# Hybrid decoder layer: memory keys computed by token, two pieces of x's last tiles split from PSUM, the first loads reordered

## The chip, the cores and the metric

The kernel runs on one core of a Trainium2 chip. The metric is the device time of one launch in microseconds, taken as the median of several runs. PE is the matrix engine (TensorE), PEld its weight loads, DVE the vector engine, ACT the scalar engine, POOL GpSimd, SP the engine whose queue issues most DMAs. SBUF is the working memory, PSUM holds the matmuls' results in eight banks.

## The reference

One layer of a decoder with three groups of heads that share one input projection, and a final norm. Sequence 1024, model width 2048, 256 memory tokens.

```
h = rmsnorm(x, ln_g)
proj = h @ w_in                      # columns of three groups
A: chunked causal gMLP gating        # 4 groups x 128
B: gated DeltaNet, 8 heads of 128    # short conv on q, k, v; chunked delta rule
C: cross-attention, 4 heads of 128:
   m = rmsnorm(mem, mem_norm_g)
   mk, mv = split(m @ w_mem_kv)      # keys, values: 256 tokens x 512 each
   p = softmax(cq @ mk.T / sqrt(128));  out = p @ mv
each group's output times silu of its own gate columns
x = x + concat(A, B, C) @ w_out
y = rmsnorm(x, final_g)
```

All of it is float32 and must come out that exactly: a product is made of three matmuls in the faster fp32r format, each operand split into a rounded part (hi) and the rest (lo): hi·hi, hi·lo, lo·hi.

## The kernel before

**The order of the work.** Every instruction is first recorded by `Plan.add`, with its dependences found from the memory regions it touches. `Plan.issue` then plays the whole program through a cost model: each engine takes, of the instructions that are ready by the model, the one with the lowest class (`rank(n)`, lower first), then the earliest in the code. `behind(op)` only tells the plan to wait for `op`. The order found is written out for each engine, and all instructions appear in the profile under line 300, so they are told apart by their tiles. On the chip each engine works its list strictly in that order and waits by semaphores.

**The first stage** computes the memory keys and values. `mem` is loaded in two tiles of 128 tokens, each in four pieces of 512 columns (`load_mem(q)` loads piece q of both; the tiles are `kT`, `qT` and their `w` twins). Seven dummy products (`warm(7)`) run on PE meanwhile. The norm weights `mem_norm_g` and `ln_g` come as 32 rows of 128 in one tile (`y1`, shown as `y`), and one PE transpose turns them into columns `gcol`. `spread_mem(q)` transposes piece q of both tiles on PE into one bank each, and splits it into hi (`gt`) and lo (`inv`). `w_mem_kv` is taken in 16 slices of 128 rows by 1024 columns (keys in the first 512, values in the rest); slice k goes into one of four buffers (`wraw`, `ut`), is scaled by its norm column and split into `whi` and `wlo`, two of each. Slice 0 is loaded and scaled in two halves, the value half first, and that half is issued on ACT's queue.

Each slice has two parts of products. For the values, `va[mt]`, memory tokens are the rows of the result: the memory tile is the stationary operand and 512 weight columns move. For the keys, `ka[h]`, the head's channels are the rows: 128 weight columns are stationary and 256 memory tokens move. `va` takes two PSUM banks (`dn0`, `dn1`), `ka` the four banks `acc0` to `acc3`. The other two (`dn2`, `dn3`, taken in turn by `spare()`) serve the transposes.

The norm of each memory token (`row_scale`, into `rm`) is applied at the end. For the values it is one number per row. For the keys, tokens lie along the free axis, so at slice 7 a product of a matrix of ones with a diagonal matrix spreads the 256 norms over all partitions (`rmb`). Keys and values then go to a DRAM buffer (`kv_d`) on POOL's queue, to be read back and split by the attention stage.

**x in the same stage.** While the slices are worked, the first half of x (tiles 0 to 3, `load_x`) is loaded into buffers that earlier work leaves. `prep` scales a tile by its row norm, piece by piece, and transposes a piece into a spare bank. `put0` multiplies it by the columns of `ln_g` (`times_g`, into `tn`), splits it into `ahi` and `alo`, and stores it to `h0_d`. For tiles 0 and 1 (`tt < H0`) it also runs a small f32 product for the decays (`decay_rows`, `first_ab`) into the unused half of a key bank.

**After it** the large projections run by a seven-product scheme (`first_product`, `seven`): its sums and differences of h are made by `left_sums`, which adds `ahi` and `alo` back together, and by `prep1` for the second half of x. The first of these products takes tiles 0 and 1 first, pieces 2 and 3, and then tiles 2 and 3. Near the end of the projections the attention stage loads keys (`mkT`) and values (`mv`) from `kv_d`.

Of the kernel before, what the change touches and what calls it, by code (L numbers as in the profile page):

```python
# [9 lines left out]
F32 = mybir.dt.float32  # L10
# [50 lines left out]
class Plan:  # L61
# [242 lines left out]
def kernel(  # L304
# [32 lines left out]
    def C(shape, name, dt=F32):  # L337
        return sb.tile(list(shape), dt, name=name, tag=name)[:]
# [72 lines left out]
    mhalf, rms = (C([P, NH], n) for n in ("mhalf", "rm"))  # L411
    rm = [rms[:, i : i + 1] for i in range(2)]
    col2 = C([P, 16], "col2")[:, 0:9]
    gcol, cw = C([P, 32], "gcol"), C([P, 96], "cw")
    jk = C([P, 2 * HT], "jk", mybir.dt.bfloat16)
    small = Ring("small", 8, [P, 8])
    acc = [ps.tile([P, HT], F32, name=f"acc{i}", tag=f"acc{i}")[:] for i in range(4)]
# [72 lines left out]
    x_rows = {}  # L490
    whole_of.update((t.tensor.name, t) for t in ring["ut"].bufs)

    def load_mem(q):
# [43 lines left out]

    turn["dn"] = 1
    warm(7)
    pt = acc[3]  # L540
    PE.transpose(pt[:, 0:32], rows[0:32], ident[0:32, 0:32])
    with rank(1):
        V.tensor_copy(gcol, pt[:, 0:32])

    def times_g(o, tp, q):
        V.tensor_tensor(out=o, in0=tp, in1=bc(gcol[:, 16 + 4 * q : 20 + 4 * q], P), op=ALU.mult)

    def spread_mem(q):
        h, l = (ring[t](F32R).rearrange("p (k n) -> p k n", k=4) for t in ("gt", "inv"))
# [35 lines left out]

    def put0(tt):
        def put(q, tp):
            t = tok(ring["tn"]())
            with rank(1):
                times_g(t, tp, q)  # L590
            with rank(2):
                split_to(ahq[q][:, tt], alq[q][:, tt], t, V)
            if tt < H0:
                decay_rows(first_ab(tt), q, t, False)
# [12 lines left out]
    for k in range(KT):  # L607
        mh, ml = mhl[k // 4]
        if k >= 4:
            with rank(3):  # L610
                load_kv(k)
        hi, lo = kvhi[k % 2], kvlo[k % 2]
        with rank(2):
            for sl in kv_parts(k)[::-1]:
                raw = kvraw[k % 4][:, sl]
                if k == 0:
                    V.tensor_scalar(hi[:, sl], raw, gcol[:, k : k + 1], None, op0=ALU.mult)
                else:
                    S.activation(hi[:, sl], raw, AF.Copy, scale=gcol[:, k : k + 1])
                V.scalar_tensor_tensor(lo[:, sl], raw, gcol[:, k : k + 1], hi[:, sl], op0=ALU.mult, op1=ALU.subtract)  # L620
        kk = k % 4
        for mt in range(2):
            sl = slice(mt * P, (mt + 1) * P)
            triple(va[mt], (mh[:, kk, sl], ml[:, kk, sl]), (hi[:, XW:], lo[:, XW:]), k == 0, k == KT - 1)
        for h in range(NX):
            sl = slice(h * P, (h + 1) * P)
            triple(ka[h][:, :NMEM], (hi[:, sl], lo[:, sl]), (mh[:, kk], ml[:, kk]), k == 0, False)
        kvmark.append(R.ops[-1])
        if k == 0:
            with behind(kvmark[-1]), rank(2):  # L630
                G.dma_start(abw[:, 0 : KT * 16].rearrange("p (k c) -> p k c", c=16),
                            w_in[:, C_AB : C_AB + 16].rearrange("(k p) c -> p k c", p=P))
        if k in (1, 4, 8):
            with behind(kvmark[-1]):
                mhl.append(spread_mem(len(mhl)))
        if k == 1:
            load_x(0, "vs", kvmark[1:2] * 4)
        if k == 3:
            for mt in range(2):
                V.tensor_copy(rm[mt], row_scale(mem_rows[mt]))  # L640
        if k == 4:
            load_x(1, "kd", kvmark[4:5] * 4)
        if k == 5:
            prep(0, put0(0), spare)
        if k == 7:

            dg, rmb = (ring["E"]()[:, 0:NMEM] for _ in range(2))
            for mt in range(2):
# [12 lines left out]
    kv_d = DT([2, NX, P, NMEM], "kvd")  # L661
    with rank(1):
# [3 lines left out]
    for h in range(NX):  # L666
        with rank(2.5):
            G.dma_start(kv_d[0, h], kfs[h])
    for mt in range(2):
        t = ring[("ai", "kd")[mt]]()  # L670
        with rank(1):
            S.activation(t, va[mt], AF.Copy, scale=rm[mt])
        with rank(2.5):
            G.dma_start(kv_d[1, :, :, mt * P : (mt + 1) * P].rearrange("h p e -> p h e"), tok(t))
    with rank(2):
        prep(3, put0(3), spare, (2, 3, 0, 1))
    sums0 = ring["xr"].bufs[1][:, 0:HT]
# [1048 lines left out]
    for n, (tag, to) in enumerate((("gt", mkT), ("inv", mv))):  # L1726
        for i in range(NX // 2):
            t = ring[tag](F32R).rearrange("p (h s m) -> p h s m", h=2, s=2)
            G.dma_start(t[:, :, 1].bitcast(F32), kv_d[n, 2 * i : 2 * i + 2].rearrange("h p m -> p h m"))
# [191 lines left out]
```

## Time and profile before

| | us |
|---|---|
| median of 3 runs | 1588.99 |
| lowest, highest | 1588.22, 1590.04 |
| profiled execution: its own time | 1590.5 |
| profiled execution: span from first to last instruction | 1588.7 |
| PE busy in the span | 1575.6 |
| DVE busy | 1287.4 |
| ACT busy | 1016.2 |

The share of TensorE's clock that was granted is 0.998 over the span. Rows of a timeline have the start and the duration in us, the engine, the operation, output<-inputs, the shape and the number of instructions merged into the row; in brackets the idle time before it, and what ended it. Matmuls overlap: a row's duration is longer than the distance to the next one's start, and that distance is what a matmul costs in a stream. Rows of the chain have start, length and number of instructions. Groups have the count, the busy time with the mean in ns of one, and the idle time before them. Rows of DMA issues have the count, the size and the median us from issue to landing. Rows of windows have the busy time and count of each engine (PE, PEld, DVE, ACT, POOL), the clock, the share of time in which the DMA engines were busy, and GB/s.

### The profile page before, as it was taken

The numbers are of one execution on the slowest core, as the hardware profiler recorded it, in microseconds if no ns is written. First come the engines' busy times: TensorE is split into PE (matmuls) and PEld (weight loads), VectorE is DVE, ScalarE is ACT, GpSimd is POOL, SyncE is SP. The second block draws the span as 40 slices with busy tenths as digits, with TensorE's granted clock in tenths as the row PEclk, the third lists the DMA queues.
The fourth block names the chain that finished last, engine by engine and source line by source line (L and its number), as shares of the span: only waits on it lengthen the run. The fifth ranks groups of instructions, "written<-read, shape, count | busy, mean of one in ns | idle before, by whom it ended". The sixth has DMA issues, their size and how long they took to land.

```text
span 1588.7 us, 25645 instructions
## 1 busy us (share of the span) xinstructions
PE 1575.6 (99%) x8762; PEld 1317.2 (83%) x8762; DVE 1287.4 (81%) x1961; ACT 1016.2 (64%) x2088; POOL 311.7 (20%) x513
## 2 busy tenths in 40 slices
PE   9999999999999999999999999999999999999997
PEld 8878888888888888888888888888888888888886
DVE  5868996989899998997988776777768788688775
ACT  6762685776656788866775667766566864344355
POOL 1200042332402424235343133121000000000001
PEclk9999999999999999999999999999999999999999
DMA  8988868988679868986779775798877779688646
GB/s 305 319 279 278 274 214 306 349 303 268 199 253 345 270 215 283 357 306 219 263 233 356 240 259 188 242 327 257 283 255 260 260 238 355 198 283 294 202 146 238
DMA packets 213219, 425.77 MB, mean 268 GB/s; under 512 B 23112, under 2 KB 58672, under 8 KB 213088
## 3 DMA queue, kind: packets, MB, share of 16 engines
q1 hardware_dynamic: 190464, 367.40, 68.9%
q0 software_dynamic: 21840, 55.40, 10.5%
q8 instruction: 69, 1.13, 0.3%
q10 hardware_dynamic: 784, 1.33, 0.2%
q14 instruction: 62, 0.51, 0.1%
HBM read 335.40 MB, written 88.11 MB: 267 GB/s over the span
## 4 chain that ended last, share of the span: by engine, by line
PE 98%; DMA 1%; DVE 0%; issue 0%; ACTq 0%; ACT 0%; POOLq 0%; POOL 0%; DVEq 0%
PE acc L300 69%; PE dn L300 29%; DMA wraw<-in_w_in_dram 0%; DMA wraw<-in_w_mem_kv_dram 0%; DVE alo L300 0%; DVE zl L300 0%; ACTq L300 0%; ACT y2w L300 0%; DVE tn L300 0%; DVE kd L300 0%; DVE vs L300 0%; DVE inv L300 0%; POOLq L1916 0%; POOL small L300 0%; DVE whi L300 0%
## 5 line engine op out<-in xcount | busy, mean ns | idle before, releaser
L300 PE MATMUL acc<-ahi,whi 128*128 128x512 f32 (+1 forms) x1328 | 455.6, 392 | 0.0
L300 PE MATMUL acc<-ahi,wlo 128*128 128x512 f32 (+1 forms) x904 | 355.0, 393 | 0.0
L300 PEld LDWEIGHTS acc<-ahi,whi 128*128 128x128 f32 x1328 | 247.8, 188 | 47.7
L300 ACT CAST ahi<-raws 128x1024 fp32r<-128x1024 f32 x141 | 147.9, 1049 | 86.7 <-PE dn L300 40.4
L300 PEld LDWEIGHTS acc<-ahi,wlo 128*128 128x128 f32 x904 | 170.0, 188 | 32.6 <-issue 0.2
L300 PE MATMUL acc<-alo,whi 128*128 128x512 f32 (+1 forms) x480 | 187.5, 391 | 0.0
L300 PE MATMUL acc<-ahi,zh 128*128 128x512 f32 x424 | 167.2, 394 | 0.0
L300 PE MATMUL acc<-ahi,zl 128*128 128x512 f32 x424 | 167.2, 394 | 0.0
L300 PE MATMUL acc<-alo,zh 128*128 128x512 f32 x424 | 167.1, 394 | 0.0
L300 ACT CAST whi<-wraw 128x1024 fp32r<-128x1024 f32 (+1 forms) x78 | 80.6, 1033 | 70.4 <-PE acc L300 42.8
L300 DVE TENSOR_TENSOR wlo<-wraw,whi 128x1024 fp32r<-128x1024 f32 (+1 forms) x78 | 93.6, 1200 | 25.5 <-ACT whi L300 22.0
L300 POOL TENSOR_TENSOR small<-small,mhalf 128x1 f32<-128x1 f32 x26 | 16.6, 643 | 491.1 <-DVE small L300 488.9
L300 DVE TENSOR_TENSOR alo<-raws,ahi 128x1024 fp32r<-128x1024 f32 x71 | 87.5, 1233 | 21.9 <-ACT ahi L300 21.7
L300 PEld LDWEIGHTS acc<-alo,whi 128*128 128x128 f32 x480 | 90.3, 188 | 17.4
L300 DVE TENSOR_TENSOR ahi<-raws,ahi 128x1024 fp32r<-128x1024 f32 x70 | 85.4, 1220 | 18.8 <-ACT ahi L300 17.3
L300 DVE TENSOR_TENSOR alo<-y,ahi 128x1024 fp32r<-128x1024 f32 x65 | 79.3, 1220 | 17.4 <-ACT ahi L300 17.1
L300 PEld LDWEIGHTS acc<-ahi,zl 128*128 128x128 f32 x424 | 79.7, 188 | 15.3
L300 PEld LDWEIGHTS acc<-ahi,zh 128*128 128x128 f32 x424 | 79.8, 188 | 15.3
L300 PEld LDWEIGHTS acc<-alo,zh 128*128 128x128 f32 x424 | 79.7, 188 | 15.2
L300 ACT CAST ahi<-y 128x1024 fp32r<-128x1024 f32 x65 | 68.2, 1049 | 37.3 <-PE dn L300 17.6
L300 PE MATMUL dn<-whi,ahi 128*128 128x512 f32 x232 | 77.6, 389 | 0.0
L300 PE MATMUL acc<-whi,ahi 128*128 128x512 f32 x216 | 73.6, 392 | 0.0
(582 smaller groups left out, 3744.8 us busy)
## 6 DMA issues: line engine op xcount, KB each, us to landing
wraw<-in_w_in_dram SPq DMA_DIRECT2D x80, 512.0 KB, 5.1
raws<-sa SPq DMA_DIRECT2D x61, 512.0 KB, 5.3
y<-in_w_in_dram SPq DMA_DIRECT2D x40, 512.0 KB, 5.2
wraw<-in_w_out_dram SPq DMA_DIRECT2D x32, 512.0 KB, 4.9
raws<-h0d SPq DMA_DIRECT2D x29, 512.0 KB, 6.0
y<-sa SPq DMA_DIRECT2D x27, 512.0 KB, 4.8
raws<-sd SPq DMA_DIRECT2D x42, 256.0 KB, 2.9
raws<-hTd SPq DMA_DIRECT2D x16, 512.0 KB, 5.2
```

The lines of the kernel that those rows point to most:

```text
L300: o.fn(*o.args, **o.kw)
```

## The change

- First loads: memory tile 0, piece 0; the memory norm; slice 0 of the weights in its two halves; only then tile 1's piece 0 and `ln_g`. The norm columns are made in two transposes: `gcol` (memory) at the start, `lcol` (`ln_g`) behind slice 0. Slice 0's key half is scaled and rounded on ACT, its value half stays on DVE. The sums of squares of the memory rows are planned behind slice 0.
- Keys by token: the keys are computed like the values, memory tile stationary, 512 key columns moving, into `acc0` and `acc1`. Their norm is then one number per row, so the spreading product goes. They are stored by token (`key_d`), and the attention stage transposes them on PE, four 128x128 blocks into each of two banks, before it splits them. The decays of tiles 0 and 1 get `acc2` and `acc3`.
- x's tiles 2 and 3, pieces 0 and 1: no `tn`, no store in `put0`. Each block of 128 is scaled by its column and rounded on ACT straight from the bank, and DVE makes the rest in one instruction. `left_sums` has hi + lo anyway and stores it to `h0_d`, and takes one more buffer there so that the sum stays whole for the store.
- x's tile 3 is loaded at slice 10, behind slices 9 and 10, where it was at slice 13, behind slices 10 to 12.

```diff
-    gcol, cw = C([P, 32], "gcol"), C([P, 96], "cw")
+    gcol, lcol, cw = C([P, 16], "gcol"), C([P, 16], "lcol"), C([P, 96], "cw")
...
+    grow = rows[32:48]
     with rank(2):
-        load_mem(0)
+        load_mem(0, 0)
         S.dma_start(mrow, mem_norm_g[0].rearrange("(c p) -> c p", p=P))
-        S.dma_start(rows[16:32], ln_g[0].rearrange("(c p) -> c p", p=P))
-        for k in range(4):
+        load_kv(0)
+        load_mem(0, 1)
+        S.dma_start(grow, ln_g[0].rearrange("(c p) -> c p", p=P))
+        for k in range(1, 4):
...
+    def columns(o, g, pt, i):
+        with rank(1):
+            PE.transpose(pt[:, 0:16], g, ident[i : i + 16, i : i + 16])
+            V.tensor_copy(o, pt[:, 0:16])
...
     def first_ab(tt):
-        return ka[tt][:, NMEM : NMEM + P]
+        return ka[2 + tt][:, 0:P]
...
         def put(q, tp):
+            if tt >= H0 and q < NQ // 2:
+                with rank(2):
+                    h, l = ahq[q][:, tt], alq[q][:, tt]
+                    for k in range(4):
+                        g = lcol[:, 4 * q + k : 4 * q + k + 1]
+                        S.activation(h[:, k], tp[:, k], AF.Copy, scale=g)
+                        V.scalar_tensor_tensor(l[:, k], tp[:, k], g, h[:, k], op0=ALU.mult, op1=ALU.subtract)
+                return
...
-                if k == 0:
+                if k == 0 and sl.start:
                     V.tensor_scalar(hi[:, sl], raw, gcol[:, k : k + 1], None, op0=ALU.mult)
...
-        for h in range(NX):
-            sl = slice(h * P, (h + 1) * P)
-            triple(ka[h][:, :NMEM], (hi[:, sl], lo[:, sl]), (mh[:, kk], ml[:, kk]), k == 0, False)
+        for mt in range(2):
+            sl = slice(mt * P, (mt + 1) * P)
+            triple(ka[mt], (mh[:, kk, sl], ml[:, kk, sl]), (hi[:, 0:XW], lo[:, 0:XW]), k == 0, k == KT - 1)
         kvmark.append(R.ops[-1])
         if k == 0:
+            with behind(kvmark[-1]):
+                columns(lcol, grow, acc[3], 32)
...
-        if k == 7:
-
-            dg, rmb = (ring["E"]()[:, 0:NMEM] for _ in range(2))
-            for mt in range(2):
-                V.tensor_scalar(dg[:, mt * P : (mt + 1) * P], ident, rm[mt], None, op0=ALU.mult)
-            pt = spare()
-            PE.matmul(pt[:, 0:NMEM], ones, dg, start=True, stop=True)
-            S.copy(rmb, pt[:, 0:NMEM])
...
+        if k == 10:
+            load_x(3, "qT", (kvmark[9], kvmark[9], kvmark[10], kvmark[10]))
         if k == 13:
-            load_x(3, "qT", (kvmark[10], kvmark[11], kvmark[11], kvmark[12]))
...
-        kfs = [t[:, i * NMEM : (i + 1) * NMEM] for t in et for i in range(2)]
-        for h in range(NX):
-            V.tensor_tensor(out=kfs[h], in0=ka[h][:, :NMEM], in1=rmb, op=ALU.mult)
...
+    for mt in range(2):
+        with rank(1):
+            V.tensor_scalar(et[mt], ka[mt], rm[mt], None, op0=ALU.mult)
         with rank(2.5):
-            G.dma_start(kv_d[0, h], kfs[h])
+            G.dma_start(key_d[mt], et[mt])
...
-        V.tensor_tensor(out=a, in0=d, in1=a, op=ALU.subtract)
-        for i, t in ((1, a), (0, d), (2, c)):
+        b = a
+        if tt >= H0:
+            Q.dma_start(rows_of(h0_d, q, tt), twos_of(a))
+            b = room()
+        V.tensor_tensor(out=b, in0=d, in1=a, op=ALU.subtract)
+        for i, t in ((1, b), (0, d), (2, c)):
...
+            if n == 0:
+                G.dma_start(raw, key_d[:, :, i * NMEM : (i + 1) * NMEM].rearrange("t p c -> p t c"))
+                d = dnr()
+                with rank(1.5):
+                    for h in range(2):
+                        for m in range(2):
+                            PE.transpose(d[:, (2 * h + m) * P : (2 * h + m + 1) * P], raw[:, m, h * P : (h + 1) * P], ident)
+                src = d.rearrange("p (h m) -> p h m", h=2)
...
-                split_to(t[:, :, 0], t[:, :, 1], t[:, :, 1].bitcast(F32), V)
+                split_to(t[:, :, 0], t[:, :, 1], src, V)
```

More of the change, by code (lines that the diff above doesn't have):

```diff
@@ L491, with load_mem @@
     whole_of.update((t.tensor.name, t) for t in ring["ut"].bufs)
-    def load_mem(q):
-        for mt in range(2):
+    def load_mem(q, *mts):
+        for mt in mts or range(2):
             Q.dma_start(mem_rows[mt][q], mem[mt * P : (mt + 1) * P, q * HT : (q + 1) * HT])
@@ L539 @@
     warm(7)
[L540 to L543, printed above, removed]
+    def columns(o, g, pt, i):
+        with rank(1):
+            PE.transpose(pt[:, 0:16], g, ident[i : i + 16, i : i + 16])
+            V.tensor_copy(o, pt[:, 0:16])
+    columns(gcol, mrow, acc[3], 0)
     def times_g(o, tp, q):
-        V.tensor_tensor(out=o, in0=tp, in1=bc(gcol[:, 16 + 4 * q : 20 + 4 * q], P), op=ALU.mult)
+        V.tensor_tensor(out=o, in0=tp, in1=bc(lcol[:, 4 * q : 4 * q + 4], P), op=ALU.mult)
     def spread_mem(q):
@@ L593, in put @@
             if tt < H0:
-                decay_rows(first_ab(tt), q, t, False)
+                decay_rows(first_ab(tt), q, t, q == 0)
             with rank(5):
@@ L638 @@
         if k == 3:
-            for mt in range(2):
-                V.tensor_copy(rm[mt], row_scale(mem_rows[mt]))
+            with behind(kvmark[0]):
+                for mt in range(2):
+                    V.tensor_copy(rm[mt], row_scale(mem_rows[mt]))
         if k == 4:
@@ L655 @@
             load_x(2, "kT", (kvmark[6], kvmark[7], kvmark[7], kvmark[8]))
+        if k == 10:
+            load_x(3, "qT", (kvmark[9], kvmark[9], kvmark[10], kvmark[10]))
         if k == 13:
-            load_x(3, "qT", (kvmark[10], kvmark[11], kvmark[11], kvmark[12]))
             with rank(2):
                 prep(2, put0(2), spare, (2, 3, 0, 1))
-    kv_d = DT([2, NX, P, NMEM], "kvd")
-    with rank(1):
-        kfs = [t[:, i * NMEM : (i + 1) * NMEM] for t in et for i in range(2)]
-        for h in range(NX):
-            V.tensor_tensor(out=kfs[h], in0=ka[h][:, :NMEM], in1=rmb, op=ALU.mult)
-    for h in range(NX):
+    kv_d = DT([NX, P, NMEM], "kvd")
+    key_d = DT([2, P, XW], "keyd")
+    for mt in range(2):
+        with rank(1):
+            V.tensor_scalar(et[mt], ka[mt], rm[mt], None, op0=ALU.mult)
         with rank(2.5):
-            G.dma_start(kv_d[0, h], kfs[h])
+            G.dma_start(key_d[mt], et[mt])
     for mt in range(2):
@@ L673 @@
         with rank(2.5):
-            G.dma_start(kv_d[1, :, :, mt * P : (mt + 1) * P].rearrange("h p e -> p h e"), tok(t))
+            G.dma_start(kv_d[:, :, mt * P : (mt + 1) * P].rearrange("h p e -> p h e"), tok(t))
     with rank(2):
@@ L1728 @@
             t = ring[tag](F32R).rearrange("p (h s m) -> p h s m", h=2, s=2)
-            G.dma_start(t[:, :, 1].bitcast(F32), kv_d[n, 2 * i : 2 * i + 2].rearrange("h p m -> p h m"))
+            raw = t[:, :, 1].bitcast(F32)
+            if n == 0:
[6 more added lines that the diff above has]
+                src = d.rearrange("p (h m) -> p h m", h=2)
+            else:
+                G.dma_start(raw, kv_d[2 * i : 2 * i + 2].rearrange("h p m -> p h m"))
+                src = raw
             with rank(1.5):
-                split_to(t[:, :, 0], t[:, :, 1], t[:, :, 1].bitcast(F32), V)
+                split_to(t[:, :, 0], t[:, :, 1], src, V)
             to += [t[:, 0], t[:, 1]]
```

1 line of the change is left out of this document (removed).

## The prediction

> **What bounds the kernel now.** I read the first page first: the busy shares, then the chain of work that ended last.
>
> ```profile
> span 1588.7 us, 25645 instructions
> PE 1575.6 (99%) x8762; PEld 1317.2 (83%) x8762; DVE 1287.4 (81%) x1961; ACT 1016.2 (64%) x2088; POOL 311.7 (20%) x513
> PE 98%; DMA 1%; DVE 0%; issue 0%; ACTq 0%; ACT 0%; POOLq 0%; POOL 0%; DVEq 0%
> ```
>
> The matrix engine is busy 99% of the span and makes up 98% of the chain. A busy matmul row is not by itself proof that the engine could do no more, so I read next whom it waited for, over the whole run.
>
> ```profile
> PE dn L300 <- POOL ones L300: 1.1, 1, 1.1
> PE dn L300 <- DVE whi L300: 0.8, 1, 0.8
> PE dn L300 <- DVE ai L300: 0.6, 1, 0.6
> PE dn L300 <- DVE tn L300: 0.3, 1, 0.3
> PE dn L300 <- DVE inv L300: 0.2, 1, 0.2
> ```
>
> This is every wait of PE for another engine: 3 us in 1589, and two of the five lie in the first 8 us. So DVE, ACT, POOL and the DMA queues have nothing to give except where they make PE wait. The change is worth what it does to (1) the start, (2) the time PE needs for the same work and (3) these waits. The start, in order of time:
>
> ```profile
> 1.06 3.36 PE L300 MATMUL dn<-ones 128*128 128x128 f32 x14 [1.06 <-POOL ones L300]
> 4.52 0.45 PE L300 MATMUL dn<-ident,kT 128*128 128x128 f32 x1
> 5.08 0.28 PE L300 MATMUL acc<-ident,y 32*128 32x32 f32 x1
> 5.99 1.06 PE L300 MATMUL dn<-ident,qT 128*128 128x128 f32 x4
> 7.24 0.88 DVE L300 TENSOR_SCALAR whi<-wraw,gcol 128x512 fp32r<-128x512 f32 x2 [1.64 <-DMA wraw<-in_w_mem_kv_dram]
> 7.87 1.19 PE L300 MATMUL dn<-whi,gt 128*128 128x512 f32 x2 [0.82 <-DVE whi L300]
> 9.50 1.05 PE L300 MATMUL dn<-ones 128*128 128x128 f32 x4
> 12.27 0.63 PE L300 MATMUL dn<-wlo,gt 128*128 128x512 f32 x1
> 12.70 0.63 PE L300 MATMUL dn<-whi,inv 128*128 128x512 f32 x1
> 14.69 0.39 PE L300 MATMUL dn<-whi,inv 128*128 128x512 f32 x1
> 14.92 0.39 PE L300 MATMUL dn<-wlo,gt 128*128 128x512 f32 x1
> ```
>
> Dummies run until 4.4, then the transposes of the two memory tiles (kT, qT) and of the norm rows (y), then a hole up to the first product at 7.87, because the weight slice had not landed. The columns also show two rates: at 12 us a 512-wide matmul starts 0.43 us after the one before (12.70 - 12.27), at 15 us 0.23 us after (14.92 - 14.69). PE starts at about half rate and reaches the full one between 12.7 and 14.7; I take 13.5. The holes between 4 and 8 us add up to 1.0 us (4.42 to 4.52, 4.97 to 5.08, 7.05 to 7.87), and every us in which the full rate comes sooner is worth half a us.
>
> **The change, part by part.** Sums are against this profiled execution, whose span is 1588.7 and whose own time is 1590.5; the runs' median is 1588.99, so I carry the difference over to the median.
>
> *First loads.* What was issued when, and how long each took to land:
>
> ```profile
> 1.72 0.45 ACTq L300 DMA_DIRECT2D wraw<-in_w_mem_kv_dram  x1
> qT<-in_mem_dram SPq DMA_DIRECT2D x1, 256.0 KB, 4.5
> wraw<-in_w_mem_kv_dram ACTq DMA_DIRECT2D x1, 256.0 KB, 5.4
> wraw<-in_w_mem_kv_dram SPq DMA_DIRECT2D x1, 256.0 KB, 5.2
> y<-in_mem_norm_g_dram ACTq DMA_DIRECT2D x1, 8.0 KB, 3.3
> y<-in_ln_g_dram ACTq DMA_DIRECT2D x1, 8.0 KB, 3.7
> 2.00:4.25 2.25, 2.25 (x12) 2.12 (x10) 0.00 (x0) 1.28 (x1) 0.97 (x1) 1.00 0.85 203
> 4.25:7.00 2.75, 2.53 (x10) 1.69 (x9) 0.19 (x1) 1.31 (x3) 0.00 (x0) 1.00 1.01 370
> ```
>
> The third load of ACT's queue is issued at 1.72; each takes about 0.45 to issue, so on both queues the first go out near 0.8, the second near 1.25. Then the memory norm lands at 4.1, ln_g at 4.95, the second memory tile at 5.75, the key half of the weights at 6.9 and the value half at 7.1. The value half was third on ACT's queue, behind ln_g, which landed 0.85 us after the norm. In the new order it is second there, the key half is second on SP's, and the second memory tile comes after them. The last two columns of the window rows (DMA share, GB/s) say how soon they can land: 457 KB moved by 4.25, then 370 GB/s with the engines full. First tile and weight slice are 786 KB, so not before 5.1; shared with the second tile I take 5.6. Then 0.44 us of DVE and 0.16 of signal: first product near 6.3, not 7.87. But the four transposes of the second tile (1.06 us), which lay in the wait, now fall beside or behind that product, and a hole of about half a us before it remains, since the first tile's own transposes end near 5.7. The work stays the same, so this gains only what the holes shrink: from 1.0 to some 0.6 us, worth 0.2 (at half rate) to 0.4. The rest hangs on the clock: if the full rate comes as much sooner as the first product does (1.5 us), that is 0.75 more. Ends: 0 (loads only trade places on full DMA engines) and -2.0. I take -0.8, a little under the 1.0 of both together, because the transposes behind the first product may keep the unbroken work from starting as early. The key half of the first slice is rounded on ACT beside DVE's value half, and the memory norms' sums of squares wait for the first slice: ACT is off the chain, and they are read at 67 us. No cost.
>
> *Keys by token.* Per slice, twelve 256-wide matmuls become six 512-wide ones. The chain shows both in this stage:
>
> ```profile
> 28.51 1.43 PE acc L300 x12
> 29.94 1.38 PE dn L300 x6
> ```
>
> -0.05 us per slice; fifteen slices at full rate make -0.7 (ends 0 and -1.1). The row of norms spread over partitions goes: one f32 product, two DVE scalings, one ACT copy.
>
> ```profile
> 38.85 0.70 PE L300 MATMUL dn<-E,ones 128*128 128x256 f32 x2
> 39.48 0.43 PE L300 MATMUL acc<-tn,abw 128*32 128x128 f32 x8
> ```
>
> -0.6 (39.48 - 38.85; ends -0.45 and -0.8). The separate transpose of ln_g, a small f32 step between the first slice's products, adds 0.25 (0 to 0.4). The four key evictions on DVE become two, and six POOL stores four: off the chain. In exchange the keys must be turned round later: eight f32 128x128 transposes in two groups. Their price, from such a group between products:
>
> ```profile
> 117.40 0.66 PE L300 MATMUL dn<-ident,kTw 128*128 128x128 f32 x4
> 117.81 0.48 PE L300 MATMUL dn<-ahi,gt 128*128 128x512 f32 x1
> 118.13 0.40 PE L300 MATMUL dn<-ahi,whi 128*128 128x512 f32 x1
> ```
>
> Four take 0.41 us, and the product after them 0.32 where 0.23 is usual: 0.5 per group, +1.0 in all (0.8 to 1.3). Where do they stand? They use two banks that the scan holds last:
>
> ```profile
> 1165.94 1.03 PE L300 MATMUL dn<-ident,vs 128*128 128x128 f32 x8
> 1198.33 0.64 PE L300 MATMUL dn<-gt,xa 128*128 128x256 f32 x4
> ```
>
> The scan leaves the banks near 1168, the keys are first used at 1198: 30 us for a chain of some 5. Nobody waits, but the PE time itself is not hidden.
>
> *Two pieces of x's last tiles.* For tiles 2 and 3 and pieces 0 and 1, one DVE scaling into `tn`, one ACT cast and one DVE subtraction become four ACT and four DVE steps of 128 straight from the bank, and four h0 stores move on SP's queue to the place where `left_sums` has the rows anyway, with four more buffers from a ring of seven.
>
> ```profile
> L300 ACT ACTIVATE vs<-dn,hs 128x128 f32<-128x128 f32 x64 | 18.8, 368 | 8.4 <-issue 6.0 <-PE dn L300 2.4
> L300 DVE SCALAR_TENSOR_TENSOR steps<-dn,sc,vs 128x128 f32<-128x128 f32 x56 | 17.3, 344 | 6.0 <-PE dn L300 4.5 <-ACT vs L300 1.3
> L300 DVE TENSOR_TENSOR tn<-dn,gcol 128x512 f32<-128x512 f32 x16 | 10.6, 686 | 3.0 <-PE dn L300 3.0
> 76.56 1.26 PE L300 MATMUL dn<-ident,qT 128*128 128x128 f32 x8 [0.35 <-DVE tn L300]
> ```
>
> DVE pays 4 x 0.34 = 1.4 as before (two steps of 0.69), ACT 4 x 0.37 in place of one cast. The bank is held longer, about 2 us and not 0.7. These pieces come last of their tile and their halves are not multiplied for tens of us, so what covers it is the 12 matmuls per weight block that PE has ready; were those gone, each piece could cost 1.3 us. What it may remove is the wait in the last row: there PE has no product left until tile 3 is split, and x's tile 3 is now asked for three slices earlier. -0.35 (0 to -0.6).
>
> Sum: -0.8 - 0.7 - 0.6 + 0.25 + 1.0 - 0.35 = -1.2 us. Median 1588.99 - 1.2 = 1587.8.
>
> **The clock.** The Trainium skill, "TensorE: Matmul & The Clock Gate", Part 1, says that the array starts at half clock and is released after a busy window of about 3.4 us which runs freely, so that the point differs from run to run. The trace agrees with two rates, not with 3.4 us from the first matmul: the half rate lasts to about 13.5, some 5.6 us past the first product. By that rule the step would move by a whole window or not at all: for the clock's part of the start an estimate of 0 or -1.7 us (half of 3.4), where the sum has a value between.
>
> **Rivals.**
> A. *The full rate comes much sooner.* PE works without a hole from about 6.3, and the step falls 3 us or more earlier: -1.5 to -2 for the start, and with the other terms near their good ends (keys -0.9, norm row -0.7, turning +0.9, last wait -0.5) about -3.2: 1585.8. For it: the half rate is the largest loss in the profile. Against it: the dummies, four of them still at 9.5, did not bring it about before. Chance 0.19.
> B. *The start is hidden anyway.* DMA engines full at 1.01 give the same bytes by the same time, or the second tile's transposes, now behind the first product, break the stretch after which the full rate comes, and the step stays at 13.5. Then -0.2 for the start and nearly nothing from the rest (-0.7 - 0.6 + 0.25 + 1.0, with or without the last wait): 1588.4 to 1588.7. Against it: ln_g's 0.85 us ahead of the value half. Chance 0.13. The same page of the Trainium skill, Part 4, says that transposes do not count as busy for the clock; no run here shows it yet, and it would bring about the second of these ways.
> C. *Slower: PE stands at the key transposes.* PE's order is written out by the planner; if it puts them behind the scan's last transposes but ahead of the reads of those banks (two ACT reads, some 0.7 us each with signals about 1 us), PE stops twice for 1 us. It decides from 1.2 us of stop on: 1587.8 + 2.1 = 1589.9, and more if a neighbouring product is dragged along. Against it: PE was stopped by such things for 1.1 us in all after 10 us. Chance 0.09.
> The forecast has the remaining 0.59.
>
> **How the numbers follow.** A measurement of this kernel can tell about 0.2% from no change, 3.2 us: faster means below 1585.8, slower above 1592.2. Half of A and a little of the forecast's tail lie below: 0.16. Of C about half: 0.05. Range: 1585.2 (A with all good ends) to 1590.0 (C, or all bad ends: 0 - 0 - 0.45 + 0.4 + 1.3 - 0 = +1.2), some 0.1 left out on each side; the forecast's own is 1586.3 to 1589.0.
>
> **What would show it.** First product near 6.3 to 7.2; the start-to-start time falling from 0.42 to 0.23 before 13; six and six 512-wide matmuls per slice; no f32 product at 38 us; eight `ident` transposes between 1168 and 1198 without idle time before them; no wait of PE for `tn` at 76. I am wrong if PE's waits after 20 us grow by more than 2 us, or if the rate steps up at another point than the start of work explains.

## Result, and the profile after

The changed kernel takes 1591.63 us (median of 21 runs, 1589.29 to 1594.82), the kernel before 1589.40 in the same session (21 runs, 1587.85 to 1590.89): a ratio of 1.0014, 95% interval 1.0007 to 1.002. That is 2.2 us longer where 1.2 us shorter was forecast. By the forecast's own bound of 0.2% it is no change; the time lies above its range, and the interval excludes a gain.

The page of the changed kernel: span, busy engines, shares of the chain of waits by engine.

```profile
span 1591.7 us, 25469 instructions
PE 1574.1 (99%) x8673; PEld 1310.5 (82%) x8673; DVE 1284.1 (81%) x1965; ACT 1019.6 (64%) x2100; POOL 312.8 (20%) x511
PE 88%; DMA 6%; DVE 3%; issue 2%; ACT 0%; POOL 0%; DVEq 0%; POOLq 0%; SPq 0%; ACTq 0%
```

PE has 89 instructions less and is busy 1.5 us less (1575.6 before), yet the span is 3.0 us longer: PE stands longer. The chain says so too: 98% PE before, 88% now, with DMA and DVE in between. Whom PE waited for (us in total, times, longest), without the rows of the dummies (1.1) and of the norm rows (0.3) in the first 5 us:

```profile
PE dn L300 <- DVE whi L300: 2.0, 1, 2.0
PE acc L300 <- ACT whi L300: 1.9, 1, 1.9
PE acc L300 <- DVE y2w L300: 0.7, 1, 0.7
PE dn L300 <- DVE inv L300: 0.5, 1, 0.5
PE dn L300 <- ACT kdw L300: 0.5, 1, 0.5
PE dn L300 <- DVE tn L300: 0.4, 1, 0.4
PE dn L300 <- DVE ai L300: 0.3, 1, 0.3
PE acc L300 <- DVE wlo L300: 0.2, 1, 0.2
```

The first row is the hole before the first product. All others lie after 20 us: 4.5 us, where the kernel before had 1.1 (ai 0.6, tn 0.3, inv 0.2). The forecast named a growth by more than 2 us as the sign that it is wrong; it is 3.4. The largest, at 164 us, with the step of DVE and the cast of ACT that it hangs on:

```profile
164.18 0.96 DVE L300 TENSOR_TENSOR wraw<-kTw,wraw 128x768 f32<-128x768 f32 x1
165.23 0.83 ACT L300 CAST whi<-wraw 128x768 fp32r<-128x768 f32 x1 [6.05 <-DVE wraw L300]
166.12 0.50 PE L300 MATMUL acc<-ahi,whi 128*128 128x512 f32 x1 [1.89 <-ACT whi L300]
```

In the kernel before the same addition stood at 161.03 and PE did not wait. The start:

```profile
4.91 0.66 PE L300 MATMUL dn<-ident,kT 128*128 128x128 f32 x4
7.55 0.64 PE L300 MATMUL dn<-whi,gt 128*128 128x512 f32 x1 [1.98 <-DVE whi L300]
7.99 1.05 PE L300 MATMUL dn<-ident,qT 128*128 128x128 f32 x4
8.69 0.77 PE L300 MATMUL dn<-wlo,gt 128*128 128x512 f32 x1
...
10.97 0.46 PE L300 MATMUL acc<-wlo,gt 128*128 128x512 f32 x1
11.27 0.39 PE L300 MATMUL acc<-whi,inv 128*128 128x512 f32 x1
```

and the value half of the first weight slice (KB, us from issue to landing):

```profile
wraw<-in_w_mem_kv_dram ACTq DMA_DIRECT2D x1, 256.0 KB, 5.6
```

The first product comes at 7.55 in place of 7.87, not at 6.3: the value half, now second on ACT's queue (issued at 1.25), takes 5.6 us and lands at 6.85. The transposes of the second memory tile (qT) now come behind that product and take 0.70 us there (8.69 - 7.99). The full rate begins near 11.1 here, 13.8 in the profile before (a first stretch at full rate, from 4.27 to 7.68 us, falls for the most part into the hole). The eight key transposes stand where the forecast put them, without idle time:

```profile
1170.82 0.60 PE L300 MATMUL dn<-ident,gt 128*128 128x128 f32 x4
1171.17 0.71 PE L300 MATMUL acc<-ahi,whi 128*128 128x512 f32 x2
...
1172.42 0.60 PE L300 MATMUL dn<-ident,gt 128*128 128x128 f32 x4
1172.77 0.48 PE L300 MATMUL acc<-ahi,wlo 128*128 128x512 f32 x1
```

### The profile page after: what moved, and what is told of

Same layout as the page of the kernel before. It is cut to its first block, busy times and chain, and to the rows that moved or that the text cites. A ratio compares the mean times of both kernels' runs of the same rounds, so it can differ in the third digit from the quotient of the medians.

```text
span 1591.7 us, 25469 instructions
## 1 busy us (share of the span) xinstructions
PE 1574.1 (99%) x8673; PEld 1310.5 (82%) x8673; DVE 1284.1 (81%) x1965; ACT 1019.6 (64%) x2100; POOL 312.8 (20%) x511
## 4 chain that ended last, share of the span: by engine, by line
PE 88%; DMA 6%; DVE 3%; issue 2%; ACT 0%; POOL 0%; DVEq 0%; POOLq 0%; SPq 0%; ACTq 0%
PE acc L300 61%; PE dn L300 27%; DMA wraw<-in_w_in_dram 3%; DMA y<-in_w_in_dram 1%; DMA gt<-in_x_dram 1%; DVE wlo L300 1%; DVE alo L300 0%; DMA pd<-y 0%; DVE zl L300 0%; DVE wraw L300 0%; DMA kdw<-in_w_in_dram 0%; DMA kTw<-in_w_in_dram 0%; DMA wraw<-in_w_mem_kv_dram 0%; DVE kT L300 0%; DVE qT L300 0%
## 5 line engine op out<-in xcount | busy, mean ns | idle before, releaser
L300 ACT CAST ahi<-y 128x1024 fp32r<-128x1024 f32 x65 | 68.2, 1050 | 39.0 <-PE dn L300 17.8
```

The lines of the kernel that those rows point to most:

```text
L300: o.fn(*o.args, **o.kw)
```

## Reading all traces together

Two executions of one kernel differ by up to 6 us here, so one pair of profiles doesn't settle 2 us. For each kernel of the table (all that were run but e1 and e2), the same PE instructions were matched with those of the profile before (by names and shape, counted from the end), and the median of their differences in time taken in a few stretches. "Full from" is where the trace's clock records begin the long stretch at full rate; "corrected" takes the clock out of the column at 130-150 us (half of the difference in "full from": a product takes 0.42 us before it and 0.23 after it).

```
kernel                     full from  130-150  corrected  215-380  1100-1140   end
before                       13.76      0.00      0.00      0.00      0.00     0.00
e7  before, more PE work     12.38      0.65      1.34      0.65     -1.24    -1.24
e10 two pieces               9.93     -1.10      0.81     -1.14     -1.23    -1.23
e11 tile 3                   13.29      1.17      1.40      1.19      2.66     2.66
e15 first loads              11.39     -0.94      0.25     -0.94     -1.70    -1.70
e9  keys                      9.32      0.18      2.40      0.33     -0.11     0.81
e3  loads, keys              13.30      1.37      1.60      2.24      2.49     3.40
e4  all but loads            11.30     -1.79     -0.56      0.53     -0.15     0.77
changed                      11.10     -0.35      0.98      1.82      2.17     3.09
e12 changed, again           10.67     -1.36      0.18      0.62     -0.10     0.82
e13 changed, no turning      11.08     -1.02      0.32      0.62      0.72     0.72
e5  changed, old mid order   10.51     -1.84     -0.22     -0.48     -1.61    -0.70
e6  before, new mid order    10.36     -1.02      0.68      2.81      4.45     4.47
e8  changed, more PE work    10.04      0.32      2.18      1.08      1.31     2.22
e14 changed, early kTw       11.38     -0.65      0.54      4.62      5.73     6.64
e16 all but keys             13.24      2.95      3.21      2.92      3.80     3.80
e17 changed, early loads     11.52     -1.22     -0.10      1.18      1.40     2.32
e18 before, longer wait       9.53      2.34      4.45      2.34      2.42     2.42
```

The correction can be tested: e7 is the kernel before with 12 transposes more, and its corrected offset is 1.34 where 1.3 was expected; e6 and e18, in which nothing is changed up to 100 and 75 us, stand at +0.13 and +0.18, corrected, between 30 and 60 us. The larger values in the corrected column are mostly PE's waits up to there: 1.72 us in e11, 1.85 in e3 and 2.57 in e9, where the kernel before has 0.35. A profile stands for one execution only: that of e11 ends 2.66 late, its median just 0.2.

## The experiments

Each is given with its edit, the expectation on record, its median with the ratio to the kernel before in the same session (95% interval), and what follows. Theory 1 was at first that the parts save what was forecast and that the planner's new order of everything downstream loses it; theory 2 that the parts themselves cost; theory 3, formed after e4, that PE comes sooner to work that DVE and the loads set, and waits there.

**The order of instructions (e1, e2, e5, e6).** The planner writes its order by `o.at`; here a list written out takes its place.

```
-        self.ops.sort(key=lambda o: (o.at, o.idx))
+        self.ops.sort(key=lambda o: place[o.idx])
```

> The changed kernel, but every instruction behind the start is issued in the place that the planner gave it in the kernel before (the same instructions, another order on each engine). Theory 1, the order: the parts save about what was forecast, and the planner's new order downstream loses it again in waits at 71-85, 164 and 383 us; then this kernel stands at 1587 to 1588.5 (0.9988 of before), without the 1.9 us wait for whi at 164. Theory 2, the content: splitting two pieces from PSUM and the key transposes themselves make PE wait, whatever the order; then it stays at 1591 to 1592 (1.0012).

> The mirror of the run before: the kernel before, but with the changed kernel's order downstream. Theory 1, the order: it gets the waits at 164 and 383 us and rises by 2 to 4 us, to 1591 to 1593 (1.002). Theory 2, the content: within 0.5 us of before.

e1: 1602.04, 1.0084 (1.007 to 1.0098). e2: 1604.20, 1.0096 (1.0081 to 1.0111). Both miss every theory. In e1 some 10 us and in e2 some 8 go between 85 and 130 us without a wait that accounts for them (e1, PE in order of time):

```profile
106.13 1.03 PE L496 MATMUL dn<-ahi,abw 128*32 128x256 f32 x12
107.09 0.50 PE L496 MATMUL dn<-ahi,wlo 128*128 128x512 f32 x1
107.53 0.62 PE L496 MATMUL dn<-ahi,abw 128*32 128x256 f32 x4
108.08 0.50 PE L496 MATMUL acc<-ahi,inv 128*128 128x512 f32 x1
108.51 0.63 PE L496 MATMUL dn<-ahi,abw 128*32 128x256 f32 x4
```

The list tore apart groups of small f32 products (`together`) and put one rounded 512-wide product after every four: four and one take 0.98 us (108.51 - 107.53). Twelve small ones in a row take 0.96 (107.09 - 106.13), so that four should cost 0.32. Neither run tells the theories apart. With the groups kept whole, and only the plan between 100 and 1050 us exchanged:

> The changed kernel with its own order up to 100 us of the plan and from 1050 us, and between them every engine's instructions in the order of the kernel before, groups kept whole. Theory 1 (order): the waits at 164 (1.9 us) and 383 us (0.7) go and do not come back elsewhere: 1588.5 to 1589.5. Theory 3 (start and scan's begin are bound by DVE and the DMA queues, so that PE that comes earlier only waits): the waits move to another place between 100 and 230 us, 1590.5 to 1592.

> The kernel before with the changed kernel's order between 100 and 1050 us of the plan. Theory 1: it takes over the waits at 164 and 383 us, +2 to +3: 1591 to 1592. Theory 3: the wait at 164 is smaller, as PE comes there later than in the changed kernel: +0 to +1, 1589 to 1590.

e5: 1591.66, 1.0011 (1.0003 to 1.002), no different from the changed kernel's 1591.63, as theory 3 expected. In its profile the waits at 158 to 164 us are 0.6 us together and that at 383 is gone, and this execution ends at -0.70 (1589.66, the second fastest of eleven); the median doesn't follow it. So the runs don't show that the wait at 164 is what they lose. e6: 1594.89, 1.0032 (1.002 to 1.0044), with waits of 1.23, 1.48 and 1.69 us, above what either theory allowed. The old order in the middle does not make the changed kernel faster: theory 1, that the new order loses what the parts won, falls as the main cause.

**More PE work at 30 us (e7, e8).**

```
+        again = [o for o in self.ops if 221 <= o.idx <= 224]   # 187 to 190 in e8
         for o in self.ops:
             o.fn(*o.args, **o.kw)
+            if o is again[-1]:
+                for o in again * 3:
+                    o.fn(*o.args, **o.kw)
```

> The kernel before, its order unchanged, with 12 more transposes of 128x128 on PE near 30 us (the first piece of x's tile 0 is turned four times in place of once): 1.3 us of PE work. PE is the bound there by the prediction: +1.0 to +1.3, 1590.0 to 1590.4. Theory 3: PE's only wait behind it is 0.35 us at 76, so that at most this much is hidden: +0.9 to +1.3.

> The changed kernel, its order unchanged, with the same 12 more transposes near 30 us. Theory 3: PE waits 1.3 us or more at 71-85 and 1.9 at 164 for work of DVE and for loads that do not depend on it, so the extra work fills these waits: 0 to +0.4, 1591.5 to 1592. Theory 1: the waits hang on the order and move with PE: +1.0 to +1.3, 1592.6 to 1593.

e7: 1590.22, 1.0006 (0.9998 to 1.0015), as expected within its interval. e8: 1594.65, 1.0037 (1.0024 to 1.005), 3.0 above the changed kernel, where theory 3 wanted 0.4 at most and theory 1 1.3. Its profile shows what theory 3 wanted, the wait at 164 down from 1.89 to 0.50 us, but that at 85 up from 0.46 to 0.84; no trace shows where the rest of the 3.0 is, and it stays open. So the run that tests theory 3 most directly bears it out in its trace and speaks against it by its time.

**One part at a time (e9, e10, e11, e15), and one left out (e3, e4, e16).** Edits are those parts of the diff; the planner plans each anew. In e15 and e16 ln_g follows the value half on ACT and both norm rows are turned in one transpose.

> Keys by token alone (products by token, no row of norms, eight transposes behind the scan); first loads, splits and tile 3 as before. The planner plans it anew. If the keys' part is what costs: +1.0 for the transposes is paid for certain, and the -1.3 in the slices is lost again in waits at 71-85 us and 164 us, as PE comes sooner to work that DVE and the loads set: 1590 to 1592. If it is worth what was forecast (-0.7 -0.6 +1.0): 1589.1.

> The two pieces of x's tiles 2 and 3 split from PSUM, and their four h0 stores moved behind the scan's start, alone. If this part costs: the bank is held 2 us longer and PE waits at 70-85, 1590 to 1591.5. If it is free, as forecast: 1589 to 1589.4, waits of PE as before (0.35 at 76).

> x's tile 3 asked for at slice 10 in place of 13, alone. If it is what was forecast: the 0.35 us wait for tn at 76 goes, 1588.7 to 1589.1. If the 256 KB loads asked for earlier only push others back, a wait moves to 80-170 us: 1589.4 to 1591.

> The first loads alone in the new order: one memory tile, its norm, the two halves of the first weight slice, then ln_g and the second memory tile; both norm rows are still turned in one transpose, keys by head as before, key half rounded on ACT. By the accounting of the traces (first product 0.5 sooner, but four transposes moved behind it, the clock's step anywhere between 9.3 and 13.8 either way): 1589.0 to 1589.6. If the two differences of runs hold (keys with loads less keys alone -1.9, change less change without loads -0.8): 1587.3 to 1588.4.

> Only the new order of the first loads and keys by token; no split from PSUM, tile 3 of x asked for at slice 13 as before. The planner plans it anew. Theory 1, the order: the saving of the start and the keys (about -1.5) plus whatever its own order costs, 0 to +4: 1587.5 to 1591.5. Theory 2, the content: without the split from PSUM the waits at 71-85 us go, 1588 to 1589.

> The change without its new order of first loads: keys by token, the two pieces from PSUM, tile 3 of x at slice 10. The full clock should come near 13.7 us as before and the first product at 7.9. Both theories: it is slower than the changed kernel by what the start gained, 0.5 to 1.5 us, 1592 to 1593, if the order downstream is the same; theory 1 allows 1588 to 1593, since the planner plans it anew.

> First loads, two pieces from PSUM and tile 3 at slice 10, but keys by head as before. If keys by token carry the loss: not slower than before by more than 0.5, 1588.5 to 1589.8, no wait at 164. If the other parts carry a share through the new order: 1590.5 or more.

```
                               median     ratio (95%)
e9  keys by token alone        1593.27    1.0026 (1.0018 to 1.0035)
e10 two pieces alone           1589.76    1.0010 (1.0001 to 1.0019)
e11 tile 3 at slice 10 alone   1589.35    1.0002 (0.9993 to 1.0011)
e15 first loads alone          1589.09    1.0000 (0.9991 to 1.0009)
e3  loads and keys             1591.36    1.0016 (1.0007 to 1.0025)
e4  all but the loads          1592.37    1.0020 (1.0012 to 1.0029)
e16 all but the keys           1593.39    1.0018 (1.0008 to 1.0027)
```

Keys by token lose most when alone: +4.1, forecast -0.3, more than either expectation had. Tile 3 and the loads of e15 can't be told from zero (within 2 us), and the two pieces lose 0.6 by the medians, 1.6 by the ratio (e10 and e11 come out between their two expectations). But the loss is not the keys' alone, and the parts don't add: e16, which leaves the keys out, is 3.9 slower than before, where 0.5 at most was expected if the keys carried the loss. PE there waits 2.1 us for the weights of the late slices and then runs 3.4 us at half rate (below). In e3, which has no split from PSUM, PE waits 1.85 us at 73 to 79, so that the split is not what makes the waits there: theory 2 falls in this. In e11 the wait for `tn` at 76 is gone, as forecast, but PE waits 0.47 us at 80 and 0.97 at 85 instead.

e15 does not have the start of the changed kernel. Both norm rows are turned at once, so that the weights' norm columns, too, wait for ln_g, which now lands later, and the first product comes later than before:

```profile
7.47 0.21 PE L300 MATMUL acc<-ident,y 32*128 32x32 f32 x1 [1.79 <-DMA y<-in_ln_g_dram]
8.93 1.20 PE L300 MATMUL dn<-whi,gt 128*128 128x512 f32 x2
```

In e9 PE ends its products at 70 us, before anything of x's tile 3 is scaled, and then stands four times:

```profile
70.94 0.66 PE L300 MATMUL dn<-ident,qTw 128*128 128x128 f32 x4 [0.68 <-DVE qTw L300]
71.94 0.66 PE L300 MATMUL dn<-ident,qTw 128*128 128x128 f32 x4 [0.34 <-DVE qTw L300]
72.94 0.66 PE L300 MATMUL dn<-ident,qT 128*128 128x128 f32 x4 [0.34 <-DVE tn L300]
74.52 0.39 PE L300 MATMUL acc<-ahi,inv 128*128 128x256 f32 x1 [0.92 <-ACT ahi L300]
```

2.3 us for DVE and ACT, in place of 0.35 at 76 us before. That and the transposes (0.92 between 1140 us and the end in the table) are 2.9 of the 3.0 by which this profile is behind at equal clock (0.81 and half of 13.76 - 9.32). Its run is the third fastest of eleven (1591.16); where the median loses 1 us more is not shown.

**The changed kernel again (e12).**

> The changed kernel once more, for a second profile. Theory 3 (PE comes sooner to work that others set): the waits at 71-85 us (1.1 us) and at 164 us (0.2 or more) are there again, with other sizes; the full clock may come anywhere between 10 and 14 us. If the waits were an accident of one execution, they are gone, and the time is still 1591.6.

1591.62, 1.0015 (1.0006 to 1.0024), and in its profile:

```profile
PE acc L300 <- ACT whi L300: 1.8, 1, 1.8
PE dn L300 <- DVE whi L300: 1.0, 1, 1.0
PE dn L300 <- DVE tn L300: 0.4, 1, 0.4
PE acc L300 <- DVE wlo L300: 0.2, 1, 0.2
```

The wait at 164 us is no accident, nor are the two at 71 to 73 (tn, wlo). Those at 85 and 383 us come and go.

**Without turning (e13).** `src = raw` in place of the eight transposes.

> The changed kernel without the eight transposes that turn the keys behind the scan (the keys are split as they lie, so they are used unturned; that part of the computation is left out). If the traces' +0.96 is their price: 1591.6 - 1.0 = 1590.6, offset at 1180 us against 1140 us zero. If the key part costs through something else behind the scan: more than -1.5.

1590.46, 1.0006 (0.9997 to 1.0015): 1.2 below the changed kernel, with intervals that overlap. In the trace the offset stays at 0.72 over that stretch, where the kernels with the transposes lose 0.91 or 0.92. The price is theirs.

**The wait at 164 us (e14, e17).** Planned times of a few instructions are set by hand: in both, `y<-kTw` and the two kTw loads come sooner and the addition to `kdw` later; in e14 the additions to `wraw` also come ahead of most of the decays (sct).

```
+        moved = {1654: 146450.0, 1715: 148150.0, 1716: 148200.0, 1717: 153000.0, 1740: 154000.0, 1875: 160000.0}
+        # e17: {1654: 146450.0, 1715: 148150.0, 1716: 148200.0, 1875: 157000.0}
+        for o in self.ops:
+            o.at = moved.get(o.idx, o.at)
```

> The changed kernel with the planner's order except for four instructions of DVE and two loads of SP near 150-160 us: the buffer of the late weight piece (kTw) is freed first and its loads are issued ahead of two stores, the addition that PE's whi waits for comes ahead of the decays, as in the kernel before. If the wait at 164 (1.8 us) is made by this order: it falls below 0.5 and the time to 1590.0-1590.6. If PE is there simply ahead of the loads: the wait stays above 1 us or moves on to the next piece before 175 us, 1591.2-1591.8.

> The changed kernel with one addition of DVE (y<-kTw) two places sooner, so that the buffer is free and the two kTw loads are issued ahead of two stores, and one addition (kdw) behind whi's; the decays stay ahead. If the wait at 164 (1.4 to 1.9 us) is made by the order on DVE and SP: below 0.5 us, no new wait on the decays, 1590.0 to 1590.6. If the loads are late anyway, since the DMA engines are full there: above 1 us, 1591.3 to 1592.

e14: 1595.63, 1.0041 (1.0029 to 1.0054). e17: 1592.68, 1.0022 (1.0013 to 1.0031). What PE waits for there, first in e14, then in e17:

```profile
164.45 0.49 PE L303 MATMUL acc<-ahi,whi 128*128 128x512 f32 x1 [0.41 <-ACT whi L303]
167.53 0.41 PE L303 MATMUL dn<-sc,utri 128*128 128x32 f32 x2 [2.59 <-DVE sc L303]
```

```profile
162.58 0.83 ACT L303 CAST whi<-wraw 128x768 fp32r<-128x768 f32 x1 [4.21 <-DVE wraw L303]
166.62 0.50 PE L303 MATMUL acc<-ahi,wlo 128*128 128x512 f32 x1 [1.73 <-DVE wlo L303]
```

In both, whi is there in time or nearly, and PE waits all the same: in e14 for the decays, which had been put behind, in e17 for wlo, which DVE makes behind it. DVE itself has waited there for a load (e17):

```profile
163.87 0.96 DVE L303 TENSOR_TENSOR wraw<-inv,wraw 128x768 f32<-128x768 f32 x1 [1.27 <-DMA inv<-in_w_in_dram]
```

So e14's wait moves on, as its second expectation says, and e17's stays above 1 us, as its second one says, but both times are longer than these allowed (by 3.8 and 0.7 us). PE is ahead of DVE and of the loads there, as theory 3 has it, and moving one thing sooner makes the next one late.

**A longer wait at 76 us (e18).** The eviction that PE waits for there in the kernel before is done five times.

```
         for o in self.ops:
-            o.fn(*o.args, **o.kw)
+            for _ in range(5 if o.idx == 629 else 1):
+                o.fn(*o.args, **o.kw)
```

> The kernel before with one eviction of DVE (tn<-dn,gcol, 0.6 us) done five times in place of once at 75.8 us, where PE waits 0.35 us for it: the wait becomes about 2.7 us. If a wait costs only itself: +2.4, 1591.8, runs in one group of 3 us as before. If a stretch of 3.4 us at half clock follows a wait of over 2 us: +2.4 and +1.7 on top in those runs where it falls into one clock window, median up to 1593.5, runs in two groups.

1592.96, 1.0024 (1.0015 to 1.0033). Windows of the profile (busy time of PE, PEld, DVE, ACT, POOL, then the granted clock):

```profile
74.00:77.80 3.80, 0.55 (x5) 0.32 (x4) 3.66 (x6) 0.29 (x1) 0.00 (x0) 1.00 1.04 387
77.80:81.21 3.41, 3.41 (x18) 3.32 (x17) 3.41 (x10) 1.55 (x3) 1.01 (x2) 0.50 1.06 394
81.21:90.00 8.79, 8.79 (x69) 8.35 (x67) 5.71 (x11) 7.63 (x12) 0.64 (x1) 1.00 0.67 213
```

The wait became 3.25 us (2.9 more), and then 3.41 us ran at a clock of 0.50. Matched PE instructions stand 1.93 us earlier than before ahead of it and 2.34 later behind it: 4.27 in all, 1.4 more than the wait itself. The wait was longer than intended, so the median says less than the trace. The two groups of runs that were expected are not seen (nine of ten between 1591.3 and 1594.5). The same stretch follows the 2.59 us in e14 and the 2.09 us in e16:

```profile
165.00:168.40 3.40, 0.87 (x6) 0.75 (x7) 3.16 (x11) 2.11 (x5) 0.00 (x0) 1.00 1.02 377
168.40:171.80 3.40, 3.40 (x10) 2.72 (x9) 3.40 (x4) 1.65 (x2) 0.00 (x0) 0.50 0.87 307
```

```profile
64.40:67.80 3.40, 1.31 (x8) 1.00 (x7) 3.30 (x7) 3.37 (x7) 0.00 (x0) 1.00 0.82 299
67.85:71.25 3.40, 3.40 (x12) 2.82 (x12) 2.11 (x6) 1.63 (x4) 1.38 (x2) 0.50 0.84 267
```

None follows the waits of 1.89 (changed kernel), 1.76 (e12) and 1.73 us (e17). But these lie across the edge of two windows of the clock (steps of 3.413 us from where a stretch begins in its records), with at most 1.5 us in one; the longest wait inside one window that no half rate follows is 1.62 us (e2, at 72).

## Why the prediction was wrong, step by step

**First loads, -0.8: the mechanism failed; what the loads are worth the runs don't settle.** The first product did come sooner, at 6.98 to 8.04 in nine profiles with the new head (the changed kernel's 7.55 and 7.24 among them), against 7.74 to 7.87 with the old, but the 0.70 us of transposes behind it eat that. The sum had halved this gain and then added 0.75 for a full rate 1.5 us sooner. The runs show no such link: in nine profiles with the old first loads the full rate begins at 9.3 to 13.8 (mean 11.1), in nine with those of the change at 10.0 to 13.3 (mean 11.1). e2 has the same head as the kernel before and the full rate 4 us sooner:

```profile
8.91 0.84 PE L496 MATMUL acc<-gt,whi 128*128 128x256 f32 x3
...
10.69 0.39 PE L496 MATMUL dn<-wlo,gt 128*128 128x512 f32 x1
10.92 0.39 PE L496 MATMUL dn<-whi,inv 128*128 128x512 f32 x1
```

The 13.76 of the profile before, from which the forecast worked, is the latest of all twenty profiles. The Trainium skill, "TensorE: Matmul & The Clock Gate", Part 1, has a window of 3413 ns that runs freely; the traces agree: every closed stretch at full or half rate in the clock records is 3.413 us or a whole multiple of it (1570.131 us = 460 windows in the profile before). The prediction drew from that rule that the step moves by a whole window or not at all, and took a value between the two. Neither is what happened: with one and the same head the full rate begins at 13.76, 12.38, 10.36 and 9.77 us (before, e7, e6, e2), so that where it begins in one profile forecasts nothing for the next. What is left of the -0.8 is not settled: e15 (1589.09 against 1589.48) has another start, and by the ratios the changed kernel stands some 1.0 us below e4 and e3 some 1.6 below e9, within the intervals.

**Keys by token, -0.7 and the norm row, -0.6: mis-sized.** The f32 product at 38 us is gone, and the products are six and six. But from the first product to the matched one at 140 us, waits and half rate taken out, PE's work is 128.8 us in the kernel before (128.7 in e18, 128.9 in e11, with the same keys) and 128.8 to 129.3 in five profiles of the changed content (the changed kernel twice, e5, e13, e17), of which some 0.35 are the moved transposes (0.70 at half rate). So hardly 0.3 us was saved where -1.05 was forecast (-0.7 - 0.6 + 0.25). Part of that shows: two 256-wide products in a row take on average 2 x 122 ns and one 512-wide 241, 3 ns a pair or 18 per slice, not the 50 of the two chain rows; the medians (2 x 120 and 232) would give those 50, so that what is lost lies in single longer steps.

**No term for new waits: the step that decides, as far as the traces show.** The forecast priced PE's work and, of the waits (its third point), took one away (-0.35); that PE, coming sooner, would wait anew in later stages it put at nothing, without having read those stages. The wait at 76 stayed, in two parts (tn 0.39, wlo 0.21 at 72 to 73), another joined it at 85 in some profiles (0.46 in the changed kernel's first, 0.33 in e13), and 1.4 to 1.9 us came at 164, where the trace of before has none. Had the forecast looked there, it could have seen how little covers an earlier PE: in the kernel before (first row) DVE is busy 9.21 of 10 us from 160 to 170, and the DMA engines are full (1.05). In the changed kernel (second row) PE stands for 1.89 of these 10 us:

```profile
160.00:170.00 10.00, 10.00 (x46) 8.29 (x45) 9.21 (x17) 5.20 (x7) 0.00 (x0) 1.00 1.05 384
160.00:170.00 10.00, 8.11 (x38) 6.38 (x37) 8.64 (x19) 4.61 (x7) 0.00 (x0) 1.00 1.06 376
```

DVE's own gap there, 0.95 us before 161.19, is a wait for a load (kdw).

**Turning the keys, +1.0: right**, 0.91 to 0.92 in the traces. **Transpose of ln_g, +0.25**: there, not measured by itself. **Two pieces, no cost**: 0.6 us alone by the medians, 0.2 to 3.0 by the interval, and a wait of 0.6 at 66 us that the cover did not hide. **Rivals**: the step of the clock came 2.7 us sooner in this profile, nearly as A had it, but profiles with the old loads have it as soon, and the time did not follow. C put its stop of PE at the key transposes, where none is; its sign was right and its place wrong. B was the nearest in time, with a start worth little; what its 1588.4 to 1588.7 lacks are the waits.

**The sum as the traces give it**, from the table: at 130 to 150 us, corrected, the changed kernel stands at +0.98, +0.18 and +0.32 (its two profiles and e13), mean +0.5; from there to 215-380 it loses 2.17, 1.98 and 1.64, mean 1.9; the transposes add 0.92. That is +3.3, against +2.2 in the medians. The difference is within what waits near 383 and 620 us do from one execution to the next (e7, the order of before, stands 1.9 us lower at 1100 us than at 380). Not settled: why the wait at 164 is in every profile of the changed kernel and in e4, but neither in e9, which has the keys alone, nor in e3, e10, e11, e15 or e16. So the cause is read from the traces: there the waits and the transposes make up the loss. No run in which the wait at 164 was made shorter (e5, e8, e14) had a shorter median for it.

## What to carry to other kernels

Where PE is 99% busy, work taken from it early was worth, in these traces, only as much as the next place where DVE and the loads are nearly full let through: before summing savings, look in the windows for such stages (here DVE 9.21 of 10, the DMA engines at 1.05), and count an earlier arrival there as a wait. Don't build on where one trace has the clock step up; read it in several. And change one part at a time, but don't expect the parts to add: here the keys alone lost 4.1 us, where 0.3 was to be won, and leaving them out still lost 3.9.

## What the runs showed of the hardware

A single wait of PE of 2.1 us or more was followed by one window of 3.41 us at a clock of 0.50 in three profiles (e14, e16, e18), and waits up to 1.9 us by none, of which at most 1.62 us (e2) lay in one window: a long wait costs itself and, by an estimate from these rows (half of 3.41), up to 1.7 us on top. The Trainium skill, "TensorE: Matmul & The Clock Gate", Part 1, has the low rate come after an idle window of about 3.4 us; in these traces 2.1 us within one window were enough. Small f32 products between rounded 512-wide ones are dear: four of them and one 512-wide took 0.98 us (e1), where four in a row come to 0.32 and the 512-wide one alone takes 0.23.
